# Down projection with 16 of its 22 row tiles by seven products instead of 12, and one product moved between the token tiles

## The chip, the cores and the metric

The kernel runs on one core of one Trainium2 chip. The metric is the device time of one execution in microseconds (us); lower is better. Five engines work side by side: TensorE (PE, matmul; its weight loads are shown apart as PEld), VectorE (DVE), ScalarE (ACT), GpSimd (POOL) and SyncE (SP, which here only issues DMAs). Each has its own queue in order; they wait for each other through semaphores.

## The reference: two layers of a decoder trunk

512 tokens, width 1024, two layers. Each layer is a feed-forward half step, a mixer (a gated recurrence beside a sliding-window attention), and a second feed-forward half step:

```python
def swiglu(h, w_gate, w_up, w_down):
    return (jax.nn.silu(h @ w_gate) * (h @ w_up)) @ w_down
...
h = rms_norm(x, gn[0])
x = x + 0.5 * rms_norm(swiglu(h, w_ffn1_gate[l], w_ffn1_up[l], w_ffn1_down[l]), gn[1])
```

Everything is float32. The inner width is 2816, that is 22 row tiles of 128. The change touches only the product with `w_down`, which comes four times in the program (two layers, two feed-forward steps): (512 x 2816) times (2816 x 1024).

## The kernel before

**Numbers in two parts.** TensorE multiplies float32 values rounded to a shorter form. Each operand is therefore split into a high part (a ScalarE cast) and a low part (the rest), and each product is made of three matmuls: high by high, high by low, low by high (`mm3`, around line 114). The low part comes from a VectorE subtraction (`split`), or from a negated ScalarE copy to which a GpSimd DMA adds the source (`split_dma`, line 423).

**Weights.** `Stream` (object `ws`) brings weight blocks of 128 x 1024 in the order of its item list: `load` issues the DMA on SyncE into one of `W32` = 4 raw tiles, `split` and `quarter` make the high and low tiles (`WS` = 6 pairs, ScalarE L277 or L335, VectorE L280 or L342). Items are prepared up to `most` items ahead of the one in use, and a raw tile is given back when its last reader is through. All other tiles of 128 x 512 come from one pool of `SLOTS` = 61 (`big()`, tile name `s`). PSUM has five tiles `acc` and three `aux`.

**Order.** TensorE's order is that of the program text. The other engines are ordered by a scheduler with a cost model; instructions inside `pin` keep their order among themselves. Work that runs beside the matmuls is placed with `order.spawn` and a modelled delay (`WAIT`).

**The down projection (`down`, `fast` true).** The 512 tokens are four token tiles, the 1024 columns two halves; `y[t][h]` collects them in PSUM. Row tiles come in pairs `j`. Twelve of the 22 row tiles (`SEVEN`) go by a seven-product scheme of the Strassen-Winograd kind: tokens 0-1 and 2-3, rows 0-5 and 6-11, and the two column halves make 2 x 2 blocks, and seven products p1 to p7 (`quarters`, `product`) take the place of eight. Sums of activation blocks are made by `Late.sums` on VectorE (`quarter_sums`, L469 to L476), sums of weight blocks by `quarter` (L258). The other ten row tiles go the plain way (`both`, `piece`).

The stages, in TensorE's order:

1. Opening: five pairs of plain rows for column half 0, all four token tiles. Beside it run the sums of activations, and `aside` loads the second-half weight blocks `b22` and `b12` (3 + 3) into tiles of the common pool, "the side block" (L247).
2. The products in the order p1, p3, p7, p2, p6, p4, p5, with 6 row slices and 3 weight items each. The weight sums: p7 uses `b12 + b22`; then `t2 = raw - that` goes into tiles of its own; p6 uses `t2` and afterwards adds it to `b22` for p5; p4 uses `raw + t2`. `fetch` loads the gains and x before p5 (L690, L695).
3. One pair of plain rows for column half 1, all token tiles.
4. Tail: `last`, four pairs for column half 1, token tile by token tile. After tile t, `post(t)` adds the products' part (`half`, L748), normalizes and adds x (L767), and `norm(t)` prepares the rows of the next sub-layer (L778), which `Pre.turn` transposes on TensorE (L124, then L595 and L601) in two halves.

Of the kernel before, what the change touches and what calls it, by code (L numbers as in the profile page):

```python
# [15 lines left out]
P = 128  # L16
# [21 lines left out]
TURN = 0  # L38
SEVEN = 12
ORDER = ("p1", "p3", "p7", "p2", "p6", "p4", "p5")  # L40
HEADS = (0, 4, 1, 5, 2, 6, 3, 7)
# [3 lines left out]
def trunk(ctx: ExitStack, tc: tile.TileContext, xin, wall, gains, lbT, hgain, sinks, c_dist, c_mask, c_ident, out):  # L45
# [109 lines left out]
    class Stream:  # L155
        def __init__(self):
            self.n, self.wall = 0, 0
            self.items = []
            self.raw, self.dma = {}, 0
            self.done, self.flight = 0, 0  # L160
            self.cur, self.c = 0, 0
            self.src = {}
            self.pinned = False
            self.most = AHEAD
            self.tight, self.gate = False, None
            self.side, self.freed = [], 0

        def plain(self, n, kind="u"):
# [24 lines left out]
        def rows(self, kt, fast):  # L193
# [17 lines left out]
            if fast:  # L211

                u, n = self.n, SEVEN // 4
                for q in range(n):
                    self.src[u + q] = pieces(q, 0)
                    self.src[u + n + q] = pieces(n + q, 0)
                self.side.append(([pieces(n + q, 1) for q in range(n)], [pieces(q, 1) for q in range(n)]))
                for k in ORDER:
                    for q in range(n):
                        it = Item(k, u + q + (n if k in ("p2", "p4") else 0), 4)  # L220
                        it.base, it.q = u, q
                        self.items.append(it)
                self.n += 2 * n
            for j in lead:
                unit(j, 1)
            self.wall = u0 + kt

# [12 lines left out]

        def aside(self, pieces):

            b = []
            for ps in pieces:
                v = [big(), big()]
                for c, a in ps:
                    nc.sync.dma_start(v[c.start // S][:, c.start % S : c.start % S + 2 * P], a)  # L247
                b.append(v)
            return b

        def quarter(self, it):

            n, q, h = SEVEN // 4, it.q, (slice(0, S), slice(S, D))
            self.load(it.base + n if it.kind == "p3" else it.u + 1)
# [5 lines left out]
            raw = [self.raw[it.u][:, c] for c in h] if it.kind in ("p1", "p7", "p2", "p4") else None  # L260
            if it.kind in ("p1", "p2"):
                w = raw
            elif it.kind in ("p3", "p5"):
                w = self.b22[q]
            elif it.kind == "p7":

                w = self.b12[q]
                sums(w, w, self.b22[q], ALU.add)
            elif it.kind == "p6":
                w = self.t2[q]  # L270
            else:
                w = raw
                sums(w, w, self.t2[q], ALU.add)
            it.hi = sb.tile([P, D], F32R, tag="whi", name=nm("whi"), bufs=WS)
            it.lo = sb.tile([P, D], F32R, tag="wlo", name=nm("wlo"), bufs=WS)
            for c in range(2):
                i = nc.scalar.copy(it.hi[:, h[c]], w[c])  # L277
                if self.pinned:
                    pin(i)
                pin(nc.vector.tensor_tensor(it.lo[:, h[c]], w[c], it.hi[:, h[c]].bitcast(F32), op=ALU.subtract))  # L280
# [9 lines left out]
            if it.kind in ("p7", "p4"):  # L290
                self.raw.pop(it.u)
                self.freed += 1
                self.load(self.freed + W32)

# [324 lines left out]

    class Late(Quarters):  # L620


        def __init__(self, src):
            self.src, self.n = src, SEVEN // 2
            self.x1, self.x56, self.x37, self.s = [], [], [], []

# [16 lines left out]

        def rest(self):
            for k in range(self.n, 2 * self.n):
                self.src[k] = split_dma(self.src[k])

        def more(self):
            self.x37 = None
            while self.s:  # L650
                self.x56.append(pair_split(self.s.pop(0), split_dma))

        def raw(self, half, i):
            return [cut(x, HALF[half]) for x in self.src[self.n : 2 * self.n]] if i else self.x1

    def down(src, kt, l, n, nxt, fast):
# [9 lines left out]
        js = list(range(SEVEN // 2 if fast else 0, kt // 2))  # L666
        part = {}

# [36 lines left out]
        if fast:  # L705
# [3 lines left out]
            for k in range(2 * js[0] + EARLY, kt):  # L709
                part[k] = split(src[k], hold=pin)  # L710
            for i, j in enumerate(js):
# [11 lines left out]
            more = quarters(late, y, lambda: (ready(kt), fetch()))  # L723
        else:
# [7 lines left out]
        last = js[-TAIL:]  # L732
        for j in js[:-TAIL]:
            ready(2 * j + 2 + EARLY)
            both(j, 1)
# [4 lines left out]
        ss = [small([P, 2], "ss2", 12) for _ in range(TT)]  # L740
        yg = [[big(), big()] for _ in range(TT)]

        def half(t, h):

            z = y[t][h]
            if fast:
                z = more[t][h]
                nc.vector.tensor_tensor(z, y[t][h], z, op=ALU.add)  # L748
            squares(z, ss[t][:, h : h + 1])
            nc.vector.tensor_tensor(yg[t][h], z, grow[0][:, h * S : (h + 1) * S], op=ALU.mult)  # L750

# [32 lines left out]
        ready(kt)  # L784
        for t in range(TT):
            half(t, 0)
        bs = [ws.next(8, TT) for _ in last]
        for t in range(TT):
            for j, b in zip(last, bs):
                for i in range(2):  # L790
                    piece(b, t, 1, j, i)
                    order.poll()
                ws.used(b)
                if pre and t == 3 and j == last[TURN]:
                    pre.turn(0, lambda kp: acc() if kp < 3 else aux())
                    norm(2)
            post(t)
            if not pre:
                order.spawn(leave(t))
            elif t != 2:  # L800
                norm(t)
# [5 lines left out]

    def quarters(late, y, fetch):

        def product(n, o, start, stop=True):
            x = late.operand(n)
            for k in range(late.n):
                if k % 2 == 0:
                    it = ws.whole()
                mv = [w.rearrange("p (m two c) -> p m two c", two=2, c=P)[:, :, k % 2, :] for w in (it.hi, it.lo)]
                for t in range(2):
                    mm3(o[t], cut(x[k], slice(t * P, (t + 1) * P)), mv, start and k == 0, stop and k == late.n - 1)
                    ws.used((it, 1))  # L820
                    order.poll()
            return o

# [7 lines left out]

        p = product(1, two(acc), True)
        late.x1 = None
        p1, u3, c12, c22 = (two(big) for _ in range(4))
# [4 lines left out]
        product(3, [y[t][1] for t in (0, 1)], True, False)  # L839
        p = product(7, two(acc), True)  # L840
        late.rest()
        late.more()
        add(u3, p, p1)
        product(2, [y[t][0] for t in (0, 1)], False)
        p = product(6, two(acc), True)
        add(c12, p, p1)
        add(u3, p, u3)
        product(4, [y[t][0] for t in (2, 3)], False)
        fetch()
        p = product(5, two(acc), True)  # L850
        add(c22, p, u3)
        add(c12, p, c12)
        return [[(p1, u3)[t // 2][t % 2], (c12, c22)[t // 2][t % 2]] for t in range(TT)]

# [70 lines left out]
    def fast(pre, a, start):  # L925
        def early():
            if j == FT - 1:
                for i in range(SEVEN, SEVEN + EARLY):
                    a[i] = split(a[i])

# [573 lines left out]
```

## Time and profile before

| | |
|---|---|
| median of three runs | 2088.98 us (2088.7 to 2089.83) |
| profiled execution | 2089.46 us, of which the program's span is 2087.7 us |
| matmuls | 13609 |
| granted TensorE clock | 0.999 of full speed |
| DMA, mean over the span | 151 GB/s |

The page has the busy time of each engine, the span in 40 slices, the DMA queues, the chain of work that ended last, and groups of instructions by line. Busy time of TensorE includes the overlap of successive matmuls, so the pace is read from the distance between starts. A timeline row gives start and duration in us, engine, line, operation, what is written and read, and the count of merged instructions; in brackets stands the engine's idle time before it and what ended it. Lines are those of the kernel before.

### The profile page before, as it was taken

Reading aid. Unit: us, or ns where it says so; the run is one execution under the profiler, and the core shown is the slowest. Engines: PE = TensorE matmul, PEld = TensorE weight load, DVE = VectorE, ACT = ScalarE, POOL = GpSimd, SP = SyncE. Lnnn points to the kernel's source line nnn. Section 1 sums busy time; section 2 is a strip of 40 time slices with the busy share of each in tenths; the row PEclk is TensorE's granted clock in tenths of the full one; section 3 lists DMA queues with packets and bytes.
Section 4 is the critical chain, followed back from the end, with each engine's and each line's share of the span. In section 5 each row is a group of like instructions: output and inputs, shape, how many; then the busy total and the mean of one; then the engine's idle time right before and its main releaser. Section 6 shows DMA issues by size and latency. Waiting matters only on the chain.

```text
span 2087.7 us, 36123 instructions
## 1 busy us (share of the span) xinstructions
PE 2077.4 (100%) x13609; PEld 1869.6 (90%) x13609; DVE 1607.9 (77%) x2825; ACT 1202.4 (58%) x2050; POOL 207.7 (10%) x250
## 2 busy tenths in 40 slices
PE   9999999999999999999999999999999999999998
PEld 7899988887898999998899998888778989999986
DVE  5887879766776788887988878877676758787877
ACT  6556666456354556567556666754653545666664
POOL 0111120000000011112001111100000000111120
PEclk9999999999999999999999999999999999999999
DMA  8587685312236368777648777652122553787683
GB/s 246 152 185 187 165 191 185 111 62 71 72 101 202 112 152 187 186 178 175 192 114 189 190 177 192 161 182 92 51 81 62 137 187 101 182 187 188 165 191 104
DMA packets 157007, 315.47 MB, mean 151 GB/s; under 512 B 17984, under 2 KB 75808, under 8 KB 156832
## 3 DMA queue, kind: packets, MB, share of 16 engines
q1 hardware_dynamic: 122416, 228.16, 32.8%
q0 software_dynamic: 34272, 84.95, 24.1%
q8 instruction: 107, 1.75, 0.4%
q14 instruction: 68, 0.56, 0.1%
q10 hardware_dynamic: 144, 0.05, 0.0%
HBM read 213.43 MB, written 14.73 MB: 109 GB/s over the span
## 4 chain that ended last, share of the span: by engine, by line
PE 98%; DMA 1%; ACT 0%; DVE 0%; SPq 0%; issue 0%
PE acc L114 73%; PE aux L114 23%; PE aux L124 1%; PE acc L124 1%; DMA s<-xin 0%; DMA w<-wall 0%; ACT whi L335 0%; DMA g_sb<-gains 0%; ACT s L511 0%; ACT wlo L339 0%; ACT s L441 0%; DVE s L767 0%; DVE s L512 0%; SPq L1352 0%; ACT s L610 0%
## 5 line engine op out<-in xcount | busy, mean ns | idle before, releaser
L114 PE MATMUL acc<-s,whi 128*128 128x256 f32 (+1 forms) x4976 | 1052.3, 309 | 1.3 <-ACT whi L335 0.5
L114 PEld LDWEIGHTS acc<-s,whi 128*128 128x128 f32 x4976 | 808.8, 191 | 49.6 <-issue 4.0
L114 PE MATMUL acc<-s,wlo 128*128 128x256 f32 (+1 forms) x2488 | 764.8, 307 | 0.1
L114 PEld LDWEIGHTS acc<-s,wlo 128*128 128x128 f32 x2488 | 475.1, 191 | 23.1 <-DVE wlo L342 0.4
L114 PE MATMUL acc<-whi,s 128*128 128x512 f32 x1344 | 437.6, 393 | 0.0
L335 ACT CAST whi<-w 128x512 fp32r<-128x512 f32 (+1 forms) x325 | 303.2, 938 | 173.3 <-PE acc L114 98.7
L335 ACT CAST whi<-tt 128x1024 fp32r<-128x1024 f32 x160 | 167.7, 1048 | 255.8 <-DVE tt L329 200.1
L114 PEld LDWEIGHTS acc<-whi,s 128*128 128x128 f32 x1344 | 252.3, 188 | 57.0 <-ACT whi L335 1.6
L342 DVE TENSOR_TENSOR wlo<-tt,whi 128x1024 fp32r<-128x1024 f32 x160 | 196.0, 1225 | 136.8 <-ACT whi L335 134.4
L340 POOL DMA_DIRECT2D wlo<-w x166 | 143.0, 861 | 1209.8 <-DVE wlo L342 498.5
L114 PE MATMUL acc<-wlo,s 128*128 128x512 f32 x672 | 261.9, 390 | 0.0
L342 DVE TENSOR_TENSOR wlo<-w,whi 128x1024 fp32r<-128x1024 f32 (+1 forms) x159 | 191.9, 1213 | 82.5 <-ACT whi L335 80.9
L114 PE MATMUL aux<-s,whi 128*128 128x256 f32 (+1 forms) x1296 | 239.2, 285 | 0.0
L114 PEld LDWEIGHTS aux<-s,whi 128*128 128x128 f32 x1296 | 202.7, 192 | 1.1 <-issue 0.5
L114 PE MATMUL aux<-s,wlo 128*128 128x256 f32 (+1 forms) x648 | 184.3, 284 | 0.0
L114 PE MATMUL aux<-whi,s 128*128 128x512 f32 x480 | 159.2, 390 | 0.0
L114 PEld LDWEIGHTS acc<-wlo,s 128*128 128x128 f32 x672 | 126.3, 188 | 24.7
L339 ACT ACTIVATE wlo<-w 128x1024 fp32r<-128x1024 f32 (+1 forms) x166 | 140.7, 847 | 0.0
L114 PEld LDWEIGHTS aux<-s,wlo 128*128 128x128 f32 x648 | 124.4, 192 | 0.3
L114 PEld LDWEIGHTS aux<-whi,s 128*128 128x128 f32 x480 | 90.1, 188 | 18.6
L411 ACT CAST s<-s 128x512 fp32r<-128x512 f32 (+1 forms) x148 | 76.9, 562 | 43.8 <-DVE s L470 41.4
L412 DVE TENSOR_TENSOR s<-s,s 128x512 fp32r<-128x512 f32 (+1 forms) x148 | 86.9, 620 | 17.9 <-ACT s L411 17.9
(185 smaller groups left out, 2350.2 us busy)
## 6 DMA issues: line engine op xcount, KB each, us to landing
w<-wall SPq DMA_DIRECT2D x267, 512.0 KB, 4.0
wlo<-w POOLq DMA_DIRECT2D x86, 512.0 KB, 5.3
w<-wall SPq DMA_DIRECT2D x256, 128.0 KB, 2.8
wlo<-w POOLq DMA_DIRECT2D x80, 256.0 KB, 3.3
s<-s POOLq DMA_DIRECT2D x72, 256.0 KB, 4.6
x_d<-s SPq DMA_DIRECT2D x48, 256.0 KB, 2.0
s<-wall SPq DMA_DIRECT2D x96, 128.0 KB, 4.0
s<-x_d SPq DMA_DIRECT2D x48, 256.0 KB, 4.9
```

The lines of the kernel that those rows point to most:

```text
L114: nc.tensor.matmul(o, lhsT, rhs, start=start, stop=stop)
L124: nc.tensor.transpose(o, src, ident)
L335: i = nc.scalar.copy(it.hi[:, c], w[:, c])
L339: self.hold(nc.scalar.mul(it.lo[:, c], w[:, c], -1.0))
L340: nc.gpsimd.dma_start(it.lo[:, c].bitcast(F32), w[:, c], accum_op=ALU.add)
L342: self.hold(nc.vector.tensor_tensor(it.lo[:, c], w[:, c], it.hi[:, c].bitcast(F32), op=ALU.subtract))
L411: (hold or ws.hold)(nc.scalar.copy(hi, src))
L412: ws.hold(nc.vector.tensor_tensor(lo, src, hi.bitcast(F32), op=ALU.subtract))
```

## The change

`SEVEN` goes from 12 to 16: 16 row tiles by seven products (8 slices and 4 weight items each), six the plain way (three pairs, which are at once the opening and the whole tail). The order becomes p1, p3, p7, p2, p6, p5; p4, which feeds only token tiles 2 and 3, is done in the tail between tiles 0-1 and 2-3. The weight sums stay in the side block: `t2` overwrites `b12`, and for p4 the raw block is added to it by GpSimd's DMA during p6. The splits of `Late` are made in smaller portions by a function called at each weight item of a product (`side1` to `side5`), so that tiles are taken later and given back one by one; four row tiles are split ahead into `ws.part`. The sum `z` of p1 and `y[0..1][0]` is made after p2 instead of in the tail.

```diff
-SEVEN = 12
-ORDER = ("p1", "p3", "p7", "p2", "p6", "p4", "p5")
+SEVEN = 16
+ORDER = ("p1", "p3", "p7", "p2", "p6", "p5")
...
             for j in lead:
                 unit(j, 1)
+            if fast:
+                product("p4")
...
             elif it.kind == "p7":
                 w = self.b12[q]
-                sums(w, w, self.b22[q], ALU.add)
-            elif it.kind == "p6":
-                w = self.t2[q]
+                if q == 0:
+                    sums(w, w, self.b22[q], ALU.add)
             else:
-                w = raw
-                sums(w, w, self.t2[q], ALU.add)
+                w = self.b12[q]
...
+            if it.kind == "p7" and q + 1 < it.n:
+                sums(self.b12[q + 1], self.b12[q + 1], self.b22[q + 1], ALU.add)
+            elif it.kind == "p6":
+                sums(self.b22[q], self.b22[q], w, ALU.add)
...
             if it.kind == "p7":
-                t = sb.tile([P, D], F32, tag="m" if q == 2 else "tt", name=nm("t2"), bufs=1 if q == 2 else 2)
-                self.t2.append([t[:, c] for c in h])
-                sums(self.t2[q], raw, w, ALU.subtract)
+                sums(w, raw(u + q), w, ALU.subtract)
+                leave(u + q)
             elif it.kind == "p6":
-                sums(self.b22[q], self.b22[q], w, ALU.add)
+                for o, x in zip(w, raw(v + q)):
+                    nc.gpsimd.dma_start(o, x, accum_op=ALU.add)
+                leave(v + q)
...
             for i, j in enumerate(js):
-                ws.most = (3, 2, 2, 3, 3)[i]
+                ws.most = (2, 3, 4)[i]
                 both(j, 0)
-                while len(late.s) < min(late.n, 2 * i + 2):
+                while len(late.s) < (3, 6, 8)[i]:
                     late.sums()
-                if i == 2:
-                    ws.b22 = ws.aside(b22)
-                elif i == 3:
-                    ws.b12, ws.t2 = ws.aside(b12), []
+                if i:
+                    aside(ws.b22, b22)
...
+            def side1(q):
+                if b22:
+                    aside(ws.b22, b22)
+                if q == 3:
+                    aside(ws.b12, b12)
+            def side3(q):
+                if b12:
+                    aside(ws.b12, b12)
+            def side7(q):
+                for k in (2 * q, 2 * q + 1):
+                    late.second(0, k)
+            def side2(q):
+                for k in (2 * q, 2 * q + 1):
+                    late.more(k)
+            def side6(q):
+                for k in (2 * q, 2 * q + 1):
+                    late.second(1, k)
+            def side5(q):
+                if q == 1:
+                    fetch()
+                elif q > 1:
+                    ready(2 * js[0] + 3 * q - 3)
...
-        for t in range(TT):
+        for t in range(2 if fast else TT):
             half(t, 0)
         bs = [ws.next(8, TT) for _ in last]
         for t in range(TT):
+            if fast and t == 2:
+                product(4, [y[t][0] for t in (2, 3)], False)
+                for t in (2, 3):
+                    half(t, 0)
+                t = 2
...
-                if pre and t == 3 and j == last[TURN]:
+                if pre and (t, j) == ((2, last[-1]) if fast else (3, last[TURN])):
                     pre.turn(0, lambda kp: acc() if kp < 3 else aux())
-                    norm(2)
+                    if not fast:
+                        norm(2)
             post(t)
...
-        product(6), p4 into y[2..3][0], fetch(), product(5)
+        z = y[0..1][0] + p1 (two VectorE additions), product(6), product(5)
```

The last two lines of the diff sum up the end of `quarters`. `late.second(half, k)` splits one half (256 columns) of one activation row by `split_dma`, where before `late.rest()` split whole rows; `late.more(k)` splits one of the sums for p5 and p6.

More of the change, by code (lines that the diff above doesn't have):

```diff
@@ L732, in down @@
         last = js[-TAIL:]
-        for j in js[:-TAIL]:
+        for j in js[: -len(last)]:
             ready(2 * j + 2 + EARLY)
@@ L830, in two @@
             return [f(), f()]
-        p = product(1, two(acc), True)
-        late.x1 = None
-        p1, u3, c12, c22 = (two(big) for _ in range(4))
+        side1, side3, side7, side2, side6, side5 = sides
+        p = product(1, two(acc), True, side=side1)
+        p1 = two(big)
         for t in range(2):
@@ L838, in quarters @@
             y[t][1] = aux()
[L839 to L846, printed above, removed]
+        product(3, [y[t][1] for t in (0, 1)], True, False, side=side3)
+        p = product(7, two(acc), True, side=side7)
+        u3 = add(two(big), p, p1)
+        product(2, [y[t][0] for t in (0, 1)], False, side=side2)
+        z = add(two(big), [y[t][0] for t in (0, 1)], p1)
+        p = product(6, two(acc), True, side=side6)
+        c12 = add(p1, p, p1)
         add(u3, p, u3)
[L848 to L851, printed above, removed]
+        p = product(5, two(acc), True, side=side5)
         add(c12, p, c12)
-        return [[(p1, u3)[t // 2][t % 2], (c12, c22)[t // 2][t % 2]] for t in range(TT)]
+        c22 = add(two(big), p, u3)
+        return [[(z, u3)[t // 2][t % 2], (c12, c22)[t // 2][t % 2]] for t in range(TT)], product
     def quad(pre, halves):
```

110 lines of the change are left out of this document (69 added, 41 removed).

## The prediction

> **What bounds the kernel now.** I read the page first, then who waits for whom on TensorE, then busy time by stage of the second down projection, then the instructions of that stage in order of time.
>
> ```profile
> span 2087.7 us, 36123 instructions
> PE 2077.4 (100%) x13609; PEld 1869.6 (90%) x13609; DVE 1607.9 (77%) x2825; ACT 1202.4 (58%) x2050; POOL 207.7 (10%) x250
> PE 98%; DMA 1%; ACT 0%; DVE 0%; SPq 0%; issue 0%
> ```
> ```profile
> engine line waited for: us in total, times, longest us
> PE acc L124 <- DVE s L767: 2.9, 1, 2.9
> PE aux L114 <- DVE eps_t L137: 1.1, 1, 1.1
> PE acc L114 <- ACT whi L335: 0.5, 1, 0.5
> ```
>
> The chain that ended last is TensorE for 98% of the span. Its longest wait, 2.9 us, stands once, in front of the last transposes; nothing in a down projection shows as a wait of TensorE. So time is won only by issuing fewer matmuls, and lost only where another engine, until now hidden, becomes late. The seven products are called here by the names of the order list, p1 to p7. How close the others are is read from one down projection, cut at 120, 252, 24 and 96 matmuls (first column halves of five row pairs, seven products, one more pair, the four-pair tail):
>
> ```profile
> core 0: us, PE busy (x) PEld busy (x) DVE busy (x) ACT busy (x) POOL busy (x), PEclk, DMA share, GB/s
> 931.50:958.70 27.20, 27.20 (x124) 22.62 (x123) 24.44 (x53) 18.62 (x36) 5.16 (x6) 1.00 0.75 175
> 958.70:1015.80 57.10, 57.10 (x254) 47.28 (x253) 45.66 (x73) 38.35 (x68) 10.43 (x12) 1.00 0.71 171
> 1015.80:1021.30 5.50, 5.50 (x26) 4.57 (x25) 5.50 (x7) 3.48 (x5) 0.00 (x0) 1.00 0.78 267
> 1021.30:1045.50 24.20, 24.20 (x117) 20.19 (x117) 20.48 (x42) 14.14 (x37) 0.00 (x0) 1.00 0.58 209
> ```
>
> VectorE is busy 90% of the opening and 80% of the products, ScalarE 68% and 67%; the clock is granted in full. This is the cover that everything below needs.
>
> **The change, part by part.**
>
> **Matmuls.** One 128x512 matmul costs the distance between starts, not its duration, because they overlap:
>
> ```profile
> 1023.39 0.39 PE L114 MATMUL aux<-wlo,s 128*128 128x512 f32 x1
> 1030.19 0.39 PE L114 MATMUL aux<-wlo,s 128*128 128x512 f32 x1
> ```
>
> Between these two lie ten groups of three: 6.80/30 = 0.2267 us. Before, a down projection has 10 plain rows x 4 token tiles x 2 halves x 3 = 240 and 7 products x 6 k x 2 tiles x 3 = 252, together 492. After: 6 x 24 = 144 and 7 x 8 x 6 = 336, together 480. Twelve fewer in each of four down projections is 48 x 0.2267 = 10.88 us, all of it on the path. TensorE waits for nothing here now, so no old wait can be won besides.
>
> The Trainium skill, page TensorE: Matmul & The Clock Gate, section Back-to-back issue gap, gives about 131 ns as the sustained spacing at 512 columns and about 216 ns for an isolated gap; by the first the saving would be 6.3 us, by the second 10.4 us. The row above agrees with neither, and I keep its 0.2267.
>
> **Opening on VectorE.** The first half of the plain rows shrinks from 5 pairs (27.2 us) to 3 (72 x 0.2267 = 16.3 us), while the activation sums grow from 6 to 8 sets, which the eight slices of p1 need.
>
> ```profile
> 932.31 1.22 DVE L342 TENSOR_TENSOR wlo<-w,whi 128x1024 fp32r<-128x1024 f32 x1
> 935.82 3.69 DVE L412 TENSOR_TENSOR s<-s,s 128x512 fp32r<-128x512 f32 x6
> 944.38 0.42 DVE L469 TENSOR_TENSOR s<-s,s 128x256 f32<-128x256 f32 x1
> 946.18 0.42 DVE L469 TENSOR_TENSOR s<-s,s 128x256 f32<-128x256 f32 x1
> 954.34 2.50 DVE L280 TENSOR_TENSOR wlo<-w,whi 128x512 fp32r<-128x512 f32 x4 [1.78 <-DMA s<-wall]
> 960.79 0.69 DVE L280 TENSOR_TENSOR wlo<-s,whi 128x512 fp32r<-128x512 f32 x1 [1.44 <-ACT whi L277]
> ```
>
> A 512-wide operation takes 0.60 us in a row of them ((3.69 - 0.69)/5), so a weight item's two low parts 1.2; a set of sums repeats every 1.80 us. VectorE got to the row splits 4.3 us after the opening began (935.82 - 931.5). By then it has split all but one of the five plain items (the last row before it is at 932.31); three will all be done. After the change it finds two row splits there instead of six (1.2), then eight sets (14.4) and the four items of p1 (4.8): done at 24.7 us. TensorE leaves p1 at 16.3 + 48 x 0.2267 = 27.2 us; the first item of p3 (1.2) is done at 25.9. That is 1.3 us to spare: hidden, cost 0, but the thinnest cover here. If it fails, each us is one us of TensorE.
>
> **Products on VectorE and ScalarE.** Each product goes from 36 to 48 matmuls (10.88 us) and from 3 to 4 weight items. In p3, p7, p2, p6 and p5 VectorE has 20 items of low parts (24.0), eight pairs of weight sums for p7 (9.6), four for p6 (4.8), 12 additions of products (7.2) and 6 row splits (3.6): 49.2 us in 5 x 10.88 = 54.4 us. Before, counted likewise with p4 (18 items, nine pairs in p7 and p6, three in p4, 10 additions, 6 splits), 45.6 in 6 x 8.16 = 49.0. The share falls from 93% to 90%. The sums of p4 are gone from VectorE (transfers make them), and two additions of the tail are done early. Cost 0.
>
> ```profile
> 935.08 3.21 ACT L411 CAST s<-s 128x512 fp32r<-128x512 f32 x6
> 939.15 0.71 ACT L411 CAST s<-s 128x256 fp32r<-128x256 f32 x2
> 980.66 0.86 POOL L423 DMA_DIRECT2D s<-s  x1 [7.15 <-ACT s L422]
> 981.70 0.86 POOL L423 DMA_DIRECT2D s<-s  x1 [0.18 <-issue]
> s<-s POOLq DMA_DIRECT2D x72, 256.0 KB, 4.6
> w<-wall SPq DMA_DIRECT2D x256, 128.0 KB, 2.8
> ```
>
> ScalarE takes 0.52 us for 512 columns and 0.32 for 256. Over the same five products: 20 items (21), the copies of p1 (1), 32 half-size casts (10), eight splits for p6 and p5 (8.4), six rows (3.1): 43.5 of 54.4. It is fullest in p2: 8.4 for those splits + 4.2 for four items = 12.6 in 10.9 us. The last of those eight splits is then ready 12.6 us after p2 began, plus 0.86 to issue and 4.6 to land, 18.1; its matmuls in p6 stand at 10.9 + 7 x 1.36 = 20.4 (six matmuls a slice). Spare: 2.3 us. Cost 0.
>
> GpSimd's transfers rise from 18 to 40 per down projection (8 + 8 splits, 16 half-size ones, 8 that add weights); the half-size ones land between the 2.8 of SyncE's 128 KB row and 4.6; I take 4.6, the only row of an adding transfer into these tiles. A weight-adding transfer waits for its item's low part and for a VectorE sum, and behind it in GpSimd's order stand splits for p6 and p4 (rival C). The added weights themselves are wanted only in p4, after p5 (10.9) and two tiles of the tail (8.2). Cost 0.
>
> **SyncE.** Bytes are the same: 22 blocks. Two blocks more go to the side tiles, 128 KB at a time, over the opening, p1 and p3. The second-half loads of the plain rows now wait until p6's weight-adding transfers have read their tiles; behind them on SyncE stand the fetch and the next sub-layer's loads. From the addition's issue 4.6 us pass until it has landed, and some 4 more for the load, and p5's 10.9 us lie between. Cost 0.
>
> ```profile
> s<-x_d SPq DMA_DIRECT2D x48, 256.0 KB, 4.9
> s<-wall SPq DMA_DIRECT2D x96, 128.0 KB, 4.0
> 1017.13 4.75 SPq L695 DMA_DIRECT2D s<-x_d  x8
> 1029.84 1.41 DVE L767 SCALAR_TENSOR_TENSOR s<-s,rt,s 128x512 f32<-128x512 f32 x2
> ```
>
> The fetch of gains and x (9 transfers) moves from before p5 to its second item: 8.2 us of p5, one tile of 4.1 and the first steps of `post` remain, about 14 us. Now the x loads are issued 12.7 us before their first use (1029.84 - 1017.13), land in 4.9, and tile 0's come first. Cost 0.
>
> **Tail.** Tiles 0 and 1 now take 18 matmuls (4.1 us) each, p4 10.9, tiles 2 and 3 again 4.1 each. p4 gives tiles 0 and 1 more time for `norm`. The tight place is the second transposition:
>
> ```profile
> 1053.34 0.88 DVE L778 TENSOR_SCALAR s<-s,rt 128x512 f32<-128x512 f32 x2
> 1054.47 0.60 PE L124 MATMUL acc<-ident,s 128*128 128x128 f32 x4
> 1039.49 1.51 PE L124 MATMUL acc<-ident,s 128*128 128x128 f32 x12
> 1040.83 0.60 PE L124 MATMUL aux<-ident,s 128*128 128x128 f32 x4
> 1040.86 1.23 DVE L342 TENSOR_TENSOR wlo<-w,whi 128x1024 fp32r<-128x1024 f32 x1 [0.34 <-ACT whi L335]
> ```
>
> The normalized rows are done at 1054.22 and transposed at 1054.47: 0.25 us spare, and the place in TensorE's order stays the same number of matmuls after `post(3)`. From the end of tile 2 to the end of tile 3 TensorE does 24 matmuls and the first transposition (1039.49 to 1041.43); after, 18 and the same. VectorE loses 6 x 0.2267 = 1.36 us there for the end of tile 2. It may get 1.2 back: three tail items are held instead of four, so one next weight item (1.23) can be split earlier, under p4. So 0 to 1.36 - 0.25 = 1.1 us; I take 0.4, nearer the low end because of that item. Three down projections have this: 1.2 us. The last has none; its end (2.9 us wait, transposes, store) is unchanged.
>
> **Sum.** The profiled execution took 2089.46 us (span 2087.7 and 1.8 around it). 2089.46 - 10.88 + 1.2 = 2079.8. The median of the runs, 2088.98, is 0.48 lower: 2079.3 us (2078.1 without the tail's 1.2).
>
> **The rivals.**
>
> *A, the opening runs out of VectorE.* The two waits quoted (1.78 for a side block, 1.44 for ScalarE) come back in a third less time: 3.2 - 1.3 spare = 1.9 us per down projection, 7.7 in all: 2079.3 + 7.7 = 2087.0, no change. For: 90% busy now. Against: the side blocks start earlier and in pieces, and four fewer row splits are queued. Chance 0.08.
>
> *B, SyncE waits for side tiles; slower.* There are 61 tiles of this size, and they have run out once already in this stage:
>
> ```profile
> SPq L247 <- PE aux L114: 5.7, 1, 5.7
> ```
>
> At the start of p7 I count 14 rows + 16 tiles of p3's and p7's split sums + 8 unsplit sums + 8 + 8 side tiles + 2 copies of p1 + 2 for the first half-size splits = 58. If the true count passes 61, a side load waits for tiles that p7 itself frees, and TensorE stands still for landing 4.0, sum 1.2, cast and low part 1.1: 6.3 us, 25.2 in four: 2079.3 + 25.2 = 2104.5. It decides from four tiles more than my count, or where SyncE's order puts a weight load behind such a wait. Against: p1's tiles are now given back one by one. Chance 0.13.
>
> *C, GpSimd's queue.* In p2 eight splits and eight weight-adding transfers meet: 16 x 1.04 (981.70 - 980.66) = 16.6, the first ready after two ScalarE passes (1.0), the last landing 4.6 later: 22.2 against 20.4. If all adding transfers go first, that is 1.8 us, four times: 2079.3 + 7.2 = 2086.5, no change. Against: each of them waits for VectorE first, so the splits are mostly ready sooner. Chance 0.07.
>
> The Trainium skill, page DMA: Bandwidth & Descriptors, section Anatomy of one DMA, fits 2.0 us plus bytes/436e3 (bytes per us) for a transfer of GpSimd's, 2.6 us at 256 KB; by it C would end at 20.2, in time, and cost nothing. The row of this trace has 4.6, and C stays.
>
> *D, the count does not fall* (the products are more than I read): no change, 2089. Chance 0.02.
>
> **How the numbers follow.** The forecast has 0.70, from 2077.5 (no tail loss, 0.6 of spread between runs) to 2082.4 (1.1 in each tail and a 1 us slip in one opening). The range must hold 0.8, so it reaches on through C and A: 2077.5 to 2087. Left out are B and D. About 0.2%, 4.2 us, is what a measurement of this kernel can tell from no change: faster means below 2084.8. Faster: 0.70 and about half of A, partly paid, 0.74. Same: the rest of A, with C and D, 0.13. Slower: B, 0.13.
>
> **What would show it.** Right: the page counts 13561 matmuls (13609 - 48); TensorE's waits still have no line of a down projection, and the transposition stands 0 to 1 us late; the opening shows VectorE above 95%. A would show as TensorE waiting for `s` of line L412 or `wlo` of the quarter items at p1 or p3; C as TensorE waiting for a transfer into `s` at p6; B as a long wait of SyncE's side loads for TensorE and TensorE waiting for `whi` at p7. The prediction is wrong if TensorE's waits in four down projections sum to over 6 us.

## The result, and the profile after

The change makes the kernel slower: 2159.37 us (median of 6 runs, 2158.05 to 2160.11) against 2088.97 (6 runs, 2088.7 to 2089.83); ratio 1.0336, interval 1.0323 to 1.0349. That is 70.4 us more where 9.7 us less were forecast. The page of the changed kernel, the lines that answer to those shown of before:

```profile
span 2158.3 us, 36578 instructions
PE 2096.1 (97%) x13561; PEld 1871.9 (87%) x13561; DVE 1632.0 (76%) x2889; ACT 1243.8 (58%) x2194; POOL 285.1 (13%) x338
PE 83%; DMA 6%; issue 5%; DVE 2%; ACT 2%; POOL 1%; SPq 0%; POOLq 0%; DVEq 0%; ACTq 0%
```

The 48 matmuls are gone as counted, but the chain that ended last now runs through DMA, VectorE and ScalarE as well. Who TensorE waits for, in the changed kernel (total us, times, longest):

```profile
PE acc L114 <- DMA s<-s: 27.6, 13, 3.6
PE acc L114 <- DVE wlo L293: 18.5, 3, 6.2
PE acc L124 <- DVE s L831: 6.7, 2, 4.1
PE acc L124 <- DVE s L842: 1.3, 3, 0.4
```

Neither of the first two stood in the list of before; the third did, with one wait of 2.9 us (L831 is the statement that was L767). Busy time by stage of the second down projection, same kernel: opening, p1, p3, p7, p2, **p6**, p5, token tiles 0 and 1, **p4**, tiles 2 and 3 (columns: length, then busy us of PE, PEld, DVE, ACT, POOL, granted clock, DMA share, GB/s):

```profile
950.30:966.60 16.30, 16.30 (x74) 13.50 (x73) 15.31 (x36) 10.16 (x21) 3.19 (x4) 1.00 0.54 126
966.60:977.50 10.90, 10.90 (x49) 9.01 (x48) 8.17 (x21) 7.55 (x15) 2.83 (x4) 1.00 1.01 247
977.50:988.40 10.90, 10.90 (x50) 9.02 (x49) 9.97 (x17) 9.27 (x22) 2.96 (x5) 1.00 0.83 221
988.40:999.30 10.90, 10.90 (x50) 9.03 (x49) 10.90 (x19) 7.22 (x17) 4.94 (x6) 1.00 1.12 256
999.30:1010.10 10.80, 10.80 (x49) 8.97 (x48) 9.80 (x16) 10.33 (x20) 5.48 (x9) 1.00 0.51 96
1010.10:1031.70 21.60, 15.04 (x50) 10.94 (x50) 9.32 (x15) 14.21 (x33) 13.79 (x17) 0.84 1.11 211
1031.70:1042.50 10.80, 10.80 (x49) 8.97 (x48) 7.85 (x11) 6.35 (x10) 1.67 (x2) 1.00 1.15 282
1042.50:1051.40 8.90, 8.81 (x37) 6.53 (x37) 8.55 (x15) 4.80 (x11) 0.00 (x0) 1.00 0.77 301
1051.40:1071.00 19.60, 13.45 (x50) 10.56 (x50) 13.72 (x28) 8.11 (x20) 0.00 (x0) 0.85 0.26 90
1071.00:1081.40 10.40, 10.40 (x54) 8.81 (x53) 7.66 (x14) 7.07 (x17) 0.00 (x0) 0.95 0.24 83
```

Two stages of 48 matmuls take 21.6 and 19.6 us in place of 10.9, and in both the granted clock falls. The stages ahead of p6, and p5, keep their pace; p7 and p5 do so with a DMA share of 1.12 and 1.15, so full DMA engines alone cost TensorE nothing. For all kernels below I use this measure: a stage's length, from its first matmul's start to the next stage's, less its matmuls times 0.2267 us, summed over the four down projections. In the kernel before, every stage has 0.0 by it except the last tile, where the transposes of `turn` stand (1.8 each, in all kernels, not counted here), and tiles 1 and 2 of the last down projection, where the output transposes stand (0.9 each). In the kernels below these output transposes stand in t1 or p4 and are counted there, so 1.8 of each sum is work that the kernel before has too; against it, the 1.3 us of the second transposition (last row of the waits) stand in no column. Us lost in one profiled execution of each kernel, and what the losses less 10.9 give against the measured difference to before:

| kernel | p6 | t0 | t1 | p4 | sum - 10.9 | measured |
|---|---|---|---|---|---|---|
| after | 42.4 | 5.8 | 5.8 | 27.4 | +70.5 | +70.4 |
| e1 | 4.4 | 6.2 | 5.9 | 27.1 | +32.7 | +31.8 |
| e2 | 14.8 | 8.7 | 6.0 | 27.7 | +46.3 | +47.5 |
| f1 | 40.9 | 9.5 | 4.0 | 2.3 | +45.8 | +44.9 |
| f2 | 5.2 | 11.1 | 3.1 | 1.0 | +9.5 | +8.1 |
| f3 | 5.3 | 11.6 | 0.4 | 1.8 | +8.2 | +8.0 |
| h1 | 4.2 | 0.8 | 0.0 | 7.3 | +1.4 | -1.0 |
| h2 | 2.2 | 0.9 | 0.0 | 1.8 | -6.0 | -6.5 |

(t0, t1: token tiles 0 and 1 of the tail.) So nearly the whole of the difference lies in four places of the down projection. The two large ones, in the changed kernel's order of time; first GpSimd's transfers from p2 to p6 (L437 the activation splits, L300 the weight-adding ones), then the landing times of this stretch:

```profile
1004.44 0.86 POOL L437 DMA_DIRECT2D s<-s  x1 [11.01 <-ACT s L436]
1005.49 0.86 POOL L437 DMA_DIRECT2D s<-s  x1 [0.18 <-issue]
1009.37 4.07 POOL L437 DMA_DIRECT2D s<-s  x2
1011.50 3.71 POOL L300 DMA_DIRECT2D s<-w  x2
1014.61 2.44 POOL L437 DMA_DIRECT2D s<-s  x2
1024.87 0.86 POOL L437 DMA_DIRECT2D s<-s  x1 [0.83 <-ACT whi L285]
1026.55 0.86 POOL L437 DMA_DIRECT2D s<-s  x1 [0.82 <-ACT whi L349]
```
```profile
s<-s POOLq DMA_DIRECT2D x8, 256.0 KB, 9.8
s<-w POOLq DMA_DIRECT2D x8, 256.0 KB, 11.6
s<-s POOLq DMA_DIRECT2D x8, 128.0 KB, 10.1
```

Issues that start 1.05 us apart at first stand 1.7 apart later (1026.55 - 1024.87), and a transfer lands after 10 to 12 us, not 4.6. All 24 transfers of this stretch land in the order of their issue: two splits, two weight-adding ones, and so on, then the eight of 128 KB. The sixteen of 256 KB land 1.63 us apart in the mean (the first at 1008.40, the last at 1032.81). TensorE's last wait in p6 ends with the seventh split's landing, here in the chain of work that ended last (start, us, what):

```profile
1014.61 13.12 DMA s<-s
1027.72 0.04 issue
1027.77 4.29 PE acc L114 x11
```

The eight of 128 KB all land later (1033.91 and after); no wait of p6 is for them. GpSimd's queue is also empty at first: its first transfer waits for ScalarE's copy until 5.2 us after p2 began (1004.44 - 999.26), and the DMA share is 0.16 from 999.30 to 1005.00. Then p4, VectorE and TensorE:

```profile
1063.99 0.88 DVE L842 TENSOR_SCALAR s<-s,rt 128x512 f32<-128x512 f32 x2
1064.79 1.28 DVE L293 TENSOR_TENSOR wlo<-s,whi 128x512 fp32r<-128x512 f32 x2
```
```profile
1066.13 0.80 PE L114 MATMUL acc<-wlo,s 128*128 128x512 f32 x1 [6.15 <-DVE wlo L293]
```

p4's last low part (L293) runs directly behind the last operation of token tile 1's `norm` (L842), and TensorE stands 6.15 us for it.

### The profile page after: what moved, and what is told of

Its sections match the earlier page's. It is cut to its first block, busy times and chain, and to the rows that moved or that the text cites. A ratio compares the mean times of both kernels' runs of the same rounds, so it can differ in the third digit from the quotient of the medians.

```text
span 2158.3 us, 36578 instructions
## 1 busy us (share of the span) xinstructions
PE 2096.1 (97%) x13561; PEld 1871.9 (87%) x13561; DVE 1632.0 (76%) x2889; ACT 1243.8 (58%) x2194; POOL 285.1 (13%) x338
## 4 chain that ended last, share of the span: by engine, by line
PE 83%; DMA 6%; issue 5%; DVE 2%; ACT 2%; POOL 1%; SPq 0%; POOLq 0%; DVEq 0%; ACTq 0%
PE acc L114 61%; PE aux L114 21%; DMA w<-wall 2%; DMA s<-w 2%; PE aux L124 1%; DMA s<-s 1%; DVE wlo L293 1%; PE acc L124 1%; ACT whi L285 1%; DMA s<-wall 0%; SPq L240 0%; DVE s L260 0%; DMA s<-xin 0%; ACT s L624 0%; POOL s L300 0%
## 5 line engine op out<-in xcount | busy, mean ns | idle before, releaser
L114 PEld LDWEIGHTS acc<-s,wlo 128*128 128x128 f32 x2488 | 475.2, 191 | 24.2 <-DMA wlo<-w 1.3
L114 PE MATMUL acc<-whi,s 128*128 128x512 f32 x1360 | 454.4, 403 | 27.7 <-DMA s<-s 27.6
L349 ACT CAST whi<-w 128x1024 fp32r<-128x1024 f32 (+1 forms) x309 | 287.0, 932 | 216.6 <-PE acc L114 98.9
L114 PEld LDWEIGHTS acc<-whi,s 128*128 128x128 f32 x1360 | 260.6, 193 | 94.3 <-DMA s<-s 36.0
L114 PE MATMUL acc<-wlo,s 128*128 128x512 f32 x680 | 271.3, 399 | 18.5 <-DVE wlo L293 18.5
L356 DVE TENSOR_TENSOR wlo<-w,whi 128x1024 fp32r<-128x1024 f32 (+1 forms) x143 | 171.9, 1213 | 88.1 <-ACT whi L349 86.5
L114 PEld LDWEIGHTS acc<-wlo,s 128*128 128x128 f32 x680 | 131.1, 193 | 46.0 <-DVE wlo L293 19.7
L437 POOL DMA_DIRECT2D s<-s x128 | 124.8, 1159 | 237.0 <-ACT s L425 100.5
L114 PE MATMUL aux<-whi,s 128*128 128x512 f32 x432 | 149.1, 401 | 1.1 <-ACT s L425 1.0
L293 DVE TENSOR_TENSOR wlo<-s,whi 128x512 fp32r<-128x512 f32 x160 | 102.7, 685 | 30.1 <-ACT whi L285 29.8
L114 PEld LDWEIGHTS aux<-whi,s 128*128 128x128 f32 x432 | 82.5, 192 | 24.7 <-DVE s L426 5.0
```

Of the source, the lines that this page charges most:

```text
L114: nc.tensor.matmul(o, lhsT, rhs, start=start, stop=stop)
L349: i = nc.scalar.copy(it.hi[:, c], w[:, c])
L356: self.hold(nc.vector.tensor_tensor(it.lo[:, c], w[:, c], it.hi[:, c].bitcast(F32), op=ALU.subtract))
L437: nc.gpsimd.dma_start(lo.bitcast(F32), src, accum_op=ALU.add)
```

## The experiments

**Theories.** For p6: T, the bytes of the transfers are more than the DMA engines can carry in p2 and p6; Q, their bytes do not matter, only that the weight-adding ones stand ahead of the splits in GpSimd's queue. For p4: V1, the low part of its last weight item has a fixed place on VectorE behind the norm of tiles 0 and 1; V2, it is late because something before it is.

**e1: the weight sums by VectorE.**

```diff
-                for o, x in zip(w, raw(v + q)):
-                    nc.gpsimd.dma_start(o, x, accum_op=ALU.add)
+                sums(w, w, raw(v + q), ALU.add)
```

> The eight transfers that add weights in p6 (32 in all) are replaced by VectorE sums. Theory T (the DMA engines are full: an adding transfer of 256 KB holds them about 1.7 us) and theory Q (the weight transfers stand ahead of the splits in GpSimd's queue and hold them up) both say that p6 loses its 10 us per down projection: about 42 us less in all. For p4, theory V1 (VectorE's order has the low part of p4's fourth item behind the norm of tile 1, whatever the transfers do) keeps 8 us in three down projections: about 2115 us. Theory V2 (p4 is late only because the x loads and the plain rows' loads landed late in the full DMA engines) lets that go too: about 2085 us. VectorE's 4.8 us more per p6 should cost nothing.

2120.96 us, ratio 1.0151 (1.0136 to 1.0166). p6's loss goes from 42.4 to 4.4; p4's stays (27.4, now 27.1): the two are separate, which speaks against V2. The page's queue rows, after and then e1, price a transfer:

```profile
q0 software_dynamic: 46944, 99.64, 27.5%
```
```profile
q0 software_dynamic: 42336, 91.24, 26.0%
```

(0.275 x 2158.3 - 0.260 x 2118.4)/32 = 1.33 us of all 16 engines for one weight-adding transfer of 256 KB.

**e2: the same transfers, a quarter of the bytes.** The sums are left out for 384 of 512 columns.

```diff
-                    nc.gpsimd.dma_start(o, x, accum_op=ALU.add)
+                    nc.gpsimd.dma_start(o[:, :P], x[:, :P], accum_op=ALU.add)
```

> The same weight-adding transfers in the same places, each over 128 of its 512 columns; three quarters of p4's weight sums are left out. T: each holds the engines about 0.45 us instead of 1.7, ten us less in front of p6's last splits, so the loss of p6 falls from 10 to under 3 us: about 2125 us or less. Q: the count, the waits and the order are unchanged, so p6 keeps 8 to 10 us and the time stays near 2155 us.

2136.63 us, ratio 1.0229 (1.0211 to 1.0246). That is 12 us above what T had said. But with number and order of the transfers kept, p6's loss falls from 42.4 to 14.8, and a loss in proportion to the bytes that are left would be 4.4 + (42.4 - 4.4)/4 = 13.9: nearly all of it goes by bytes (T), and Q, as put, is out. The order still counts, since the transfers land in it: what stands ahead of a split costs the time of its bytes.

**e3: the weight-adding transfers issued at p5's items.**

```diff
-                for o, x in zip(w, raw(v + q)):
-                    nc.gpsimd.dma_start(o, x, accum_op=ALU.add)
-                leave(v + q)
...
             elif it.kind == "p5":
+                for o, x in zip(self.b12[q], raw(v + q)):
+                    nc.gpsimd.dma_start(o, x, accum_op=ALU.add)
+                leave(v + q)
```

> The same transfers with all their bytes, issued with p5's items instead of p6's, so that p2's splits are alone. T: eight splits at 1.7 us are 13.6 us in p2, p6 loses 0 to 3 us; the bytes come back in p5, where they delay the loads for the tail: t0 loses some us more than now (0.7 to 2.5). Total 2115 to 2135 us. Q: p6 loses nothing. If p6 still loses over 5 us, neither the burst nor the order is the cause.

2171.11 us, ratio 1.0393 (1.0377 to 1.0408), a miss. Items are prepared up to four ahead, so the transfers were still issued from 1007 us on, among the splits; p6 lost 29.2 and p5, which had lost 0.5, 17.2. By its own expectation (p6 still loses over 5 us) neither burst nor order would be the cause, but the edit did not move the transfers as meant, so it tells nothing. Whether the splits alone ahead of the adding transfers would have been enough is not shown.

**e4: e1 with p4 back between p6 and p5** (and out of the tail).

```diff
-ORDER = ("p1", "p3", "p7", "p2", "p6", "p5")
+ORDER = ("p1", "p3", "p7", "p2", "p6", "p4", "p5")
...
+        product(4, [y[t][0] for t in (2, 3)], False)
```

> VectorE sums as in the first run, and p4 put back between p6 and p5, as in the kernel before; 16 rows by seven products stay. V1: the 8 us of p4 go, as VectorE has no norm beside it: 2080 to 2090 us. V2: the same time as the first run. If p4's splits of the second half land late there, p4 itself loses up to 5 us each.

2129.63 us, ratio 1.0196 (1.0181 to 1.0211), a miss: 8.7 us worse than e1. p4 now waits for its own activation splits (17.5 us of TensorE's waits on transfers) and without p4 in the tail the transposes of `turn` wait for the norm of tile 1 (13.8 us in three). The place in the tail is thus not the fault; it covers both.

**f1: p4's low parts without their fixed place.**

```diff
-                pin(nc.vector.tensor_tensor(it.lo[:, h[c]], w[c], it.hi[:, h[c]].bitcast(F32), op=ALU.subtract))
+                i = nc.vector.tensor_tensor(it.lo[:, h[c]], w[c], it.hi[:, h[c]].bitcast(F32), op=ALU.subtract)
+                if it.kind != "p4":
+                    pin(i)
```

> The kernel after with one edit: the low parts of p4's weights lose their fixed place in VectorE's program order; no operation is added or left out. V1 (p4 loses 8.1, 8.7 and 8.6 us in the first three down projections because its last low part stands on VectorE behind the norm of token tiles 0 and 1): these three losses go to under 1 us each, p6's 10 stay, and the time is about 2159.4 - 25 = 2134 us. V2 (p4 is late because p6's transfers are late, and with them everything behind): p4's losses stay at 8 us, and the time is 2155 to 2160.

2133.78 us, ratio 1.0213 (1.0196 to 1.023): as V1 said. p4's loss goes in the three down projections that have a norm; that the total meets 2134 so closely is in part luck, since t0 grew by 3.7 and p6 and t1 shrank by 3.2. Nothing was taken out; the last low part (1048.89) stands ahead of tile 1's addition of x (L833) and norm now:

```profile
1048.18 0.69 DVE L293 TENSOR_TENSOR wlo<-s,whi 128x512 fp32r<-128x512 f32 x1 [0.96 <-ACT whi L285]
1048.89 0.69 DVE L293 TENSOR_TENSOR wlo<-s,whi 128x512 fp32r<-128x512 f32 x1
1052.53 1.41 DVE L833 SCALAR_TENSOR_TENSOR s<-s,rt,s 128x512 f32<-128x512 f32 x2
```

**f2: e1 and f1 together.** Both edits above.

> The weight sums of p6 by VectorE instead of GpSimd's adding transfers (as e1) and p4's low parts without their fixed place (as f1). If the two losses are separate (T and V1), they add up: 2121.0 of e1 less 25 is about 2096 us, with p6 at +1, p4 under +1, and t0 at +1 to +2 in each down projection and the last one's t1 at +6 left over. If one loss only uncovers the other (a wait that both shared), p6 or t2 grows in place of p4 and the time stays over 2110.

2097.03 us, ratio 1.0039 (1.0024 to 1.0054). The two losses add up. Left are t0 (11.1, 17 short waits for the low parts of row splits, 0.6 us at most), p6 (5.2) and the last down projection's output (3.1).

**f3: f2, rows split earlier, last output later.**

```diff
-                if q == 1:
+                if q == 0:
+                    ready(2 * js[0] + 3)
+                elif q == 1:
                     fetch()
-                elif q > 1:
-                    ready(2 * js[0] + 3 * q - 3)
+                elif q == 2:
+                    ready(kt)
...
-            yield WAIT["final"]
+            yield WAIT["final"] + (6000.0 if t < 2 else 0.0)
```

> f2 with two moves in the tail: the row splits of the side tiles are placed one to two steps earlier in p5, ahead of p4's casts on ScalarE, and in the last down projection the output of token tiles 0 and 1 leaves 6000 units of the planner's time later. If t0's 0.7 to 1.8 us are the row splits behind p4's casts, t0 goes to about 0 in each (6 us together); if the 5.9 us in the last t1 are output transposes placed ahead of their data, they go to about 0: 2096 - 12 = about 2084 us, 0.2% under the kernel before (2089). If the row splits are late for want of a buffer, t0 stays and only the last 6 go: 2090.

2096.85 us, ratio 1.0036 (1.0023 to 1.0049), half a miss: the last t1 is clean (3.1 to 0.4), t0 keeps 11.6.

**f4: f3, the last two of eight pair sums split by VectorE.**

```diff
-            self.x56[k] = pair_split(self.s[k], split_dma)
+            self.x56[k] = pair_split(self.s[k], split if k > 5 else split_dma)
```

> f3 with the last two of the eight pair sums behind the opening split by VectorE instead of by two GpSimd transfers each (4 fewer transfers in a down projection). If p6's remaining 0.6 to 1.4 us are TensorE waiting for the last of these transfers, they go: about 2080 us, the count of matmuls showing in the time at last (before less 10.9 is 2078). If VectorE has no room in p2 and p6, with its sums of the weights there already, p6 keeps or raises its loss: 2084 or more.

2105.11 us, ratio 1.0076 (1.0061 to 1.0091). p6 falls from 5.3 to 1.6, as fewer transfers should give, but VectorE pays more: p5 loses 2.6 and t0 18.3. VectorE has no room left there: in the second down projection it is busy 11.70 of 11.70 us in p5 and 9.03 of 9.03 in t0.

**g1: f3, two p4 items prepared only after tile 0's matmuls** (order of the program text). **g2: g1, the weight sums by GpSimd itself. g3: g1 with 62 tiles.**

```diff
+        if fast:
+            ws.most = 0
         bs = [ws.next(8, TT) for _ in last]
...
+            ws.most = AHEAD
             post(t)
```
```diff
-                sums(w, w, raw(v + q), ALU.add)
+                for o, x in zip(w, raw(v + q)):
+                    nc.gpsimd.tensor_tensor(o, o, x, op=ALU.add)
```
```diff
-SLOTS = 61
+SLOTS = 62
```

> f3 with one edit: two of p4's three remaining weight tiles are prepared only after token tile 0's matmuls of the tail, so that their casts (ScalarE) and low parts (VectorE, four of 0.6 us between the last row splits and their matmuls in f3) no longer stand ahead of the last row splits. If t0's 2.6 to 3.8 us in f3 are this order on the two engines: t0 goes to under 0.7 in each down projection, p4 stays under +1, and the time is 2096.9 - 10 = about 2087 us. If p4's preparation is then too late behind the norm's work, p4 takes back what t0 gives: 2093 to 2100. If the row splits wait for buffers of `s`, nothing changes: 2096.

> g1 with p6's eight 128x512 weight sums in each down projection computed by GpSimd as an operation of its own, in place of VectorE (e1 to g1) and of its adding transfers (after). If p6's last 0.5 to 1.8 us per down projection come from VectorE being full there, they go: 4 us less than g1. If GpSimd is the slower hand, so that its sums hold back the transfers queued behind them (8 sums plus the transfers in p2 and p6, about 22 us of room), p6 loses several us in each: 8 to 20 us more than g1.

> g1 with 62 instead of 61 tiles of `s`, which is the most that fits. If transfers and row splits in p2, p6 and p5 start late for want of a tile, p6 and t0 each lose up to 1 us less per down projection: 2 to 6 us under g1. If order on the engines decides, the time is g1's within 1.5 us.

g1: 2096.7 us, ratio 1.0041 (1.0026 to 1.0055), a miss, and inconclusive for its question: the scheduler put p4's low parts ahead of the row splits all the same (VectorE in g1):

```profile
1016.85 1.28 DVE L902 TENSOR_TENSOR s<-acc,s 128x512 f32<-128x512 f32 x2
1018.05 2.49 DVE L293 TENSOR_TENSOR wlo<-s,whi 128x512 fp32r<-128x512 f32 x4
1020.45 1.89 DVE L427 TENSOR_TENSOR s<-s,s 128x512 fp32r<-128x512 f32 x3
```

g3: 2099.76 us, ratio 1.0047 (1.0032 to 1.0061): one more tile gains nothing. g2: 2119.39 us, ratio 1.0146 (1.0131 to 1.0161): the second branch of its expectation. GpSimd takes 1.79 us for a sum, and the transfers behind them come late (p6 21.3, t0 17.7):

```profile
L302 POOL TENSOR_TENSOR s<-s,w 128x512 f32<-128x512 f32 x32 | 54.0, 1790 | 2.9 <-DVE wlo L293 2.6
```

**h1: g1, the row splits and three of p4's four items given their places, rows first** (`both` puts the VectorE part of a split under `pin` too).

```diff
-                if self.pinned:
+                if self.pinned or it.kind == "p4" and q < 3:
                     pin(i)
...
-                if it.kind != "p4":
+                if it.kind != "p4" or q < 3:
                     pin(i)
...
-                    src[i] = split(src[i])
+                    src[i] = split(src[i], hold=pin if fast else None, both=fast)
```

> g1 left the order on the engines as it was: p4's casts and low parts still stood ahead of the last three row splits. Here both are given their places: the row splits keep their program order on ScalarE and VectorE, and so do three of p4's four weight tiles behind them (the fourth stays free). Nothing is added or left out. If t0's 2.6 us per down projection are this order, t0 goes to 0 to 1 us, p4 stays under +1 and the time is 2096.7 - 4 x 2 = about 2089 us, level with the kernel before. If the row splits were late for want of buffers, t0 stays at 2 to 3 us and the time at 2096. If p4's low parts are late behind the norm again, p4 takes 2 to 8 us in each and the time is over 2100.

2088.41 us, ratio 0.9996 (0.9986 to 1.0005), level with before. t0's loss falls from 11.8 to 0.8: it was order, not tiles. VectorE in h1:

```profile
1015.99 1.28 DVE L902 TENSOR_TENSOR s<-acc,s 128x512 f32<-128x512 f32 x2
1017.18 1.89 DVE L427 TENSOR_TENSOR s<-s,s 128x512 fp32r<-128x512 f32 x3
```

p4 loses 1.7 to 2.0 in each. In the first three down projections its low parts stand behind the norm of tile 0; in the last it is no wait (below).

**h2: h1, these items right behind the row splits. h3: h2, the last output later still.**

```diff
         bs = [ws.next(8, TT) for _ in last]
+        ws.most = AHEAD
+        ws.ahead()
...
-            ws.most = AHEAD
             post(t)
```
```diff
-            yield WAIT["final"] + (6000.0 if t < 2 else 0.0)
+            yield WAIT["final"] + (9000.0 if t < 2 else 0.0)
```

> h1 with p4's first three weight tiles placed right behind the last row splits, ahead of the norm of token tile 0, not behind token tile 0's matmuls. If p4's 1.7 to 2.0 us in h1 are its low parts behind that norm, they go in three down projections and the time is 2088.4 - 5 = about 2083 us, faster than before by 0.3%: the matmuls left out show at last. If the norm is then late for its transposes, t2 grows by what p4 gives (turn(0), 0 to 3 us each) and the time stays within 1 us of h1. In the last down projection p4 may lose up to 2.5 us more, since its output transposes wait for the same VectorE.

> h2, and in the last down projection the output transposes of token tiles 0 and 1 stand 3000 units of the planner's time later still. If the last p4's loss (1.8 us in h1) is these transposes ahead of their data, it goes, and the time is 1.5 to 4 us under h2: 2080 to 2082. If they are then late behind p4 and lengthen the end, the time is h2's or 1 to 2 us more.

h2: **2082.83 us, ratio 0.997 (0.9958 to 0.9981)**: faster than both kernels. The longest of TensorE's waits in h2:

```profile
PE acc L124 <- DVE s L834: 2.6, 1, 2.6
PE acc L124 <- DVE s L845: 1.3, 3, 0.4
```

h3: 2083.34 us, ratio 0.9974 (0.9964 to 0.9984), no gain over h2. The 1.8 in the last p4 only moved (0.9 there and 0.9 in tile 2), and it was no loss: TensorE does not wait there. It is the time of the output transposes themselves, eight for each of tiles 0 and 1, which the kernel before has at the end of tiles 1 and 2. In h2, then before:

```profile
2055.46 1.03 PE L124 MATMUL acc<-ident,s 128*128 128x128 f32 x8
2059.75 1.03 PE L124 MATMUL acc<-ident,s 128*128 128x128 f32 x8
```
```profile
2063.59 1.03 PE L124 MATMUL acc<-ident,s 128*128 128x128 f32 x8
2069.92 1.04 PE L124 MATMUL acc<-ident,s 128*128 128x128 f32 x8
```

## Why the prediction was wrong, point by point

- **The matmuls held.** 13561, and 10.88 us: by the table the losses less 10.9 meet every measured difference within 2.4 us, and h2 shows the gain with the losses cut to 4.9, of which 1.8 are the output transposes.
- **"GpSimd's transfers ... Cost 0" failed, and is the first cause** (shown by e1 and e2). The prediction has the eighth split of p2 ready 12.6 us after p2 began and landed at 18.1. In the trace it is ready at 13.8 and lands at 30.2 (1029.41 - 999.26): ScalarE's term held within 1.2 us, the landing did not. I took a landing of 4.6 us and a pitch of 1.04 as fixed; this stretch shows them only at its start. Rival C had the place and the sign right (TensorE waiting for a transfer into `s` at p6) and the price wrong: 1.8 us a time, measured 9.8 to 11.8. The term missing is the time that each transfer takes from those behind it. It stood in the page of before:

```profile
q0 software_dynamic: 34272, 84.95, 24.1%
```

  0.241 x 2087.7/84.95 = 5.92 us of all 16 engines per MB, 1.55 us per 256 KB (weight-adding ones alone: 1.33 by e1). The seventh split has twelve transfers of 256 KB ahead of it, six of them weight-adding. The first lands 9.1 us after p2 began, the seventh split is then due at 9.1 + 12 x 1.55 = 27.7, and p6 wants it at 10.9 + 6 x 1.36 = 19.0: 8.7 us too late, 9.5 measured; p6 lost 10.6 in this down projection. The 1.55 was there beforehand; the 9.1 is read afterwards. C had 1.0 + 4.6 in its place, which with 1.55 gives 24.2, or 5.2 us a time. The late start alone is not the cause: e1's first split is issued no earlier (5.8 us into p2), and its p6 loses 1.3 there.
- The Trainium skill's fit (DMA: Bandwidth & Descriptors, Anatomy of one DMA), 2.6 us at 256 KB, by which C would cost nothing, is a single transfer's time; here 9.8 and 11.6 were measured as medians with up to eight in flight.
- **The tail's term was mis-sized by omission, and is the second cause** (shown by f1). "p4 gives tiles 0 and 1 more time for `norm`" is true (e4 shows what happens without it), but I did not ask where p4's own items are prepared. Three tail items and four of p4 are seven; there are six pairs of tiles. The seventh is prepared when p4's first gives its pair back, which in the program text is behind `norm(1)`, and `pin` holds its low part to that place: 8.1 to 8.7 us, three times.
- **Not in the sum at all:** the row splits behind p4's casts and low parts (t0: 5.8 us, 11 once the larger waits were gone; h1 shows it for the latter), and the last down projection's output transposes ahead of their data (5.8 in t1, 0.9 of it the transposes themselves; f3 moves them and the wait goes).
- **Held:** the opening (0.0 lost; VectorE 15.31 of 16.30 us, 94%, where over 95% was forecast; rival A did not come), the products on VectorE and ScalarE, SyncE (no stage before p6 lost anything; rival B did not come), and the second transposition, 0.4 us three times, measured 1.3 for the 1.2 forecast. But "Cost 0" for VectorE held only with the sums on the transfers: with them on VectorE it is busy 12.15 of 12.15 us in e1's p6 (second down projection), and f4 shows it full in p5 and t0.
- The sign set for "wrong", over 6 us of TensorE's waits, came at some eight times that (27.6 + 18.5 + 6.7 + 1.3, less the wait of 2.6 at the very end that the kernel before has too).

## What to carry to other kernels

Price a transfer twice, by its landing and by its share of the engines (queue share x span / MB, from the page), and add up the second over what stands ahead, in the same queue, of the transfer that is waited for: a median landing from an idle stretch says nothing about a full one. When work is moved in a program whose order is partly fixed, follow the preparing of its operands too: count the buffers it is prepared into, find which item must wait for one, and see what stands ahead of it on its engine. A count of matmuls saved shows only when every such place is clean; here leaving out 10.9 us of matmuls made the kernel 70 us slower and, with eight sums on another engine and the same work in another order, 6.5 us faster.

## What the runs showed of the hardware

A long wait of TensorE can cost more than its length. In the changed kernel:

```profile
1020.97 1.22 PE L114 MATMUL acc<-whi,s 128*128 128x512 f32 x2 [3.63 <-DMA s<-s]
1027.77 1.22 PE L114 MATMUL acc<-whi,s 128*128 128x512 f32 x2 [2.28 <-DMA s<-s]
```
```profile
1020.00:1027.00 7.00, 4.52 (x12) 3.27 (x12) 1.29 (x2) 5.11 (x11) 3.58 (x5) 0.76 1.12 231
1027.00:1034.00 7.00, 6.23 (x21) 5.03 (x22) 2.82 (x5) 1.05 (x1) 3.62 (x5) 0.76 1.14 230
```

From the end of each of these waits the granted clock is 0.5 for 3.41 us (a mean of 0.76 over 7.00). What that costs depends on what follows. p4 lost 8.7 us with one wait of 6.15: the other 2.5 are matmuls at a slower pace. p6 lost 10.6 with 21.60 - 15.04 = 6.6 of idle time, but there the slower pace behind the first wait cost nothing, as the seventh split landed at 1027.72 in any case; only the 1.2 us behind the last wait did. The Trainium skill (TensorE: Matmul & The Clock Gate, Part 1: The HAM clock gate) has the half rate and the window of about 3.4 us; the trace agrees. Not every wait brings it: f2's 17 waits of up to 0.6 us in t0 left the clock at full speed there, and so did waits of 3.25 and 3.56 us in p6 of f1's third down projection, which lost 9.7 all the same.

GpSimd's elementwise sums slow some of VectorE's operations: beside them (g2) the longest of its low parts takes 1767 ns, in the same kernel without them (g1) 695; the median is 686 in both (ns: shortest, median, longest):

```profile
L293 DVE TENSOR_TENSOR wlo<-s,whi x160: 674/686/1767, 264.1 to 2091.7; 128x512 fp32r<-128x512 f32 x160
```
```profile
L293 DVE TENSOR_TENSOR wlo<-s,whi x160: 681/686/695, 264.1 to 2066.0; 128x512 fp32r<-128x512 f32 x160
```
